# A transformer block on one core: the first modulation by strips of TensorE, one weight ring, and an output projection that ends token tile by token tile

## The chip, the core and the metric

The kernel runs on one core of a Trainium2 chip. Its engines work side by side and wait for one another through semaphores: TensorE (PE, with its weight loads PEld), VectorE (DVE), ScalarE (ACT), GpSimd (POOL) and SyncE (SP), whose queue issues most of the DMAs. The metric is the device time of one execution in microseconds (us); less is better.

## The reference

One layer over 512 latent tokens `x` and 256 context tokens `ctx`, width 1024, all in float32. Cut to what the change touches:

```python
m_lat = (silu(c) @ mod_w + mod_b)[:, None, :]        # conditioning of the latent tokens
m_ctx = silu(c_ctx) @ mod_w + mod_b                  # and of the context tokens
sh1, sc1, g1, sh2, sc2, g2 = split(m_lat, 6)         # six sections of 1024 columns
csh1, csc1, cg1, csh2, csc2, cg2 = split(m_ctx, 6)
h_lat = rms_norm(x, norm_mix_g) * (1 + sc1) + sh1
h_ctx = rms_norm(ctx, norm_mix_g) * (1 + csc1) + csh1
z_lat, z_ctx = h_lat @ w_in, h_ctx @ w_in            # then two mixers (gated DeltaNet "A", HGRN2 "B"), four heads each, both directions: ya, yb; the gates m_a, m_b
y = (sigmoid(m_a) * (ya @ w_up_a) + sigmoid(m_b) * (yb @ w_up_b)) @ w_out
x = x + g1 * y
h = rms_norm(x, norm_ffn_g) * (1 + sc2) + sh2
gate, up = split(h @ ffn_w_in, 2)                    # 2816 columns each
x = x + g2 * ((silu(gate) * up) @ ffn_w_out)
return rms_norm(x, final_norm_g)
```

## The kernel before

Everything on TensorE has 128 partitions. The 512 latent tokens are four token tiles of 128, the width is KT = 8 tiles `d`. Activations lie transposed (features on partitions, tokens in columns). To keep float32 accuracy, both operands of a large product are split into a high and a low half (`hi`, `lo`; `hhi`, `hlo` for the latent tokens, `chi`, `clo` for the context) and multiplied in three matmuls by `mm3` (L105). `split` fetches a weight by SP's queue into `raw`, ScalarE casts it to `hi` (L95), VectorE subtracts to get `lo` (L97); each ring of such tiles has two buffers.

The order on each engine is set by a scheduler that follows the order of the code and priorities written in it (`tc.cur_priority`), and by the rings of buffers that tiles share.

**Start.** SP's queue fetches the tiles of `mod_w` (`mw`, one for each d, with shift and scale columns, 512 bytes a run), x, and the first six column tiles of `w_in` (`wr`). `norm_rows` takes the norm of the tokens. `modulation(d, s)` computes the shift and the scale of feature tile d for s = 0 (latent) or s = 1 (context): VectorE multiplies the 8 rows of tiles by the conditioning and adds them into two `macc` (L264, L266), TensorE sums over partitions by four matmuls with a vector of ones into `pmod` (L270). `mod_columns` (L272) makes `mcol`. `prepare(d)` transposes x on TensorE (`px`, L283), ScalarE applies `mcol` (L285 for `hhi`, L287 for `hf`), VectorE makes `hlo` (L288) and `wl` (L300). Then 18 matmuls `pg` for each d (L316). The six `pg` banks are gates 16 to 21; gates 22 and 23 follow (`pgate`, 24 matmuls each), and beside them `modulation(d, 1)` for the context. After them come the context's tokens (`chi`, `clo`), the small projection `pab` (L369), and from `h_z` on the mixers' heads.

**Mixers.** A written plan orders the heads. `head_norm` (L419) squares a head's output on ScalarE, scales the sum `h_ss` on VectorE (L423), raises it to the power -0.5 on POOL (L426), applies it on ScalarE (L428) and transposes on TensorE (`h__pt`, L431). In this part the other sections of the modulation are computed in `mod_quarter`: POOL's queue fetches `mwb`, VectorE adds into `acc` (L829). They and the last gates have a later priority.

**After the mixers.** `branch` and `up` make the up-projections (`pup`), whose merge gives `mh`, `ml`. The output projection `pwo` has two halves of 512 columns, each with four banks (one for each token tile g). The contraction is four weight pieces kk: two are multiplied for all token tiles, the last two token tile by token tile. Then the residual (`xt`, L1015, `x1`, L1016), its square (L1017), the norm's scale `st` (L1022 to L1024), `xn` (L1026), transposes `px` (L1030) and `hhi`, `hlo` again (L1034 to L1038). SwiGLU follows: 22 tiles f of 128 columns of gate and up (`pf`), 48 matmuls each; f = 0 runs on two halves of 256 tokens, so that it can begin on token tiles 0 and 1. The last product is `pfo`.

Of the kernel before, what the change touches and what calls it, by code (L numbers as in the profile page):

```python
# [7 lines left out]
F32 = mybir.dt.float32  # L8
# [7 lines left out]
KT = 8  # L16
# [32 lines left out]
def body(tc, T, out, tap=None):  # L49
# [8 lines left out]
    with ExitStack() as root:  # L58
# [25 lines left out]
        def split(srcs, kt, n, pool=None):  # L84
# [5 lines left out]
            for s in srcs:  # L90
                w = s.shape[1]
                nc.sync.dma_start(raw[:, :, c0:c0 + w], s.rearrange("(k p) f -> p k f", p=P))
                c0 += w
            hi = pool.tile([P, kt, n], F32R, name=f"hi{WN[0]}", tag="hi")
# [59 lines left out]
        with ExitStack() as st:  # L154
# [32 lines left out]
            def load_mod(d):  # L187
                mw = s1.tile([P, KT, 256], F32, name=f"mw{d}")
                for j in range(2):
                    nc.sync.dma_start(mw[:, :, P * j:P * j + P],  # L190
                                      T["mod_w"][0, :, D * j + P * d:D * j + P * d + P].rearrange("(k p) f -> p k f", p=P))
                mws.append(mw)

            load_mod(0)
            for g in (2, 3, 4, 5):
                load_x(g)
            for d in range(KT):
                if d > 0:
                    load_mod(d)
                wr = s1.tile([P, NG0 * P], F32, name=f"wr{d}", tag="wr", bufs=3)  # L200
                nc.sync.dma_start(wr[:, :], W_IN[P * d:P * d + P, C_MB:C_MB + NG0 * P])
                wraws.append(wr)
# [39 lines left out]

            ss = s1.tile([P, 6], F32, name="ss")
# [14 lines left out]
            def modulation(d, s):  # L258

                accs = [sp.tile([P, 256], F32, name=f"macc{d}_{s}{i}", tag=f"macc{i}", bufs=4) for i in range(2)]  # L260
                for k in range(KT):
                    acc, col = accs[k % 2], sc[:, 8 * s + k:8 * s + k + 1]
                    if k < 2:
                        nc.vector.tensor_scalar_mul(acc[:, :], mws[d][:, k, :], col)  # L264
                    else:
                        nc.vector.scalar_tensor_tensor(acc[:, :], mws[d][:, k, :], col, acc[:, :], op0=ALU.mult, op1=ALU.add)  # L266
                for j in range(2):
                    c = 16 * s + 2 * d + j
                    for i, acc in enumerate(accs):
                        nc.tensor.matmul(pmod0[:, c:c + 1], acc[:, P * j:P * j + P], ones[:, 0:1], start=(i == 0), stop=(i == 1))  # L270

            def mod_columns(s, d0, d1):  # L272

                ps = pmod0[:, 16 * s + 2 * d0:16 * s + 2 * d1].rearrange("p (d j) -> p d j", j=2)
                nc.vector.tensor_tensor(mcol[:, s, d0:d1, 0], ps[:, :, 0], mb_sh[:, d0:d1], op=ALU.add)
                nc.vector.tensor_tensor(mcol[:, s, d0:d1, 1], ps[:, :, 1], mb1[:, d0:d1], op=ALU.add)
                nc.vector.tensor_tensor(mcol[:, s, d0:d1, 1], mcol[:, s, d0:d1, 1], g_mix[:, d0:d1], op=ALU.mult)
# [13 lines left out]
            pmod0 = bank("ha", "pmod0")  # L291
# [28 lines left out]
            norm_rows((0, 1))  # L320
            cd = list(range(KT))
# [803 lines left out]
```

## Time and profile before

| what | value |
|---|---|
| median of 3 runs (lowest to highest) | 1096.97 us (1096.02 to 1098.99) |
| profiled execution | 1099.97 us |
| its span | 1098.3 us |
| mean granted TensorE clock | 0.983 |
| TensorE busy | 1034.3 us |
| VectorE / ScalarE / GpSimd busy | 699.2 / 554.6 / 75.7 us |

The span runs from the first to the last recorded instruction. Between the start of x's first projection and the end, the program passes these edges (us from the start of the span): 67.9 the gates, 100.2 the mixers, about 610 the up-projections, 659.3 the output projection, 704.7 the transposes for SwiGLU, 737.0 its third tile. Times in the prediction are those of the profiled execution; it lies 3.0 us above the median.

### The profile page before, as it was taken

The numbers are of one execution on the slowest core, as the hardware profiler recorded it, in microseconds if no ns is written. First come the engines' busy times: TensorE is split into PE (matmuls) and PEld (weight loads), VectorE is DVE, ScalarE is ACT, GpSimd is POOL, SyncE is SP. The second block draws the span as 40 slices with busy tenths as digits, with TensorE's granted clock in tenths as the row PEclk, the third lists the DMA queues.
The fourth block names the chain that finished last, engine by engine and source line by source line (L and its number), as shares of the span: only waits on it lengthen the run. The fifth ranks groups of instructions, "written<-read, shape, count | busy, mean of one in ns | idle before, by whom it ended". The sixth has DMA issues, their size and how long they took to land.

```text
span 1098.3 us, 16604 instructions
## 1 busy us (share of the span) xinstructions
PE 1034.3 (94%) x6439; PEld 856.0 (78%) x6439; DVE 699.2 (64%) x1373; ACT 554.6 (50%) x1042; POOL 75.7 (7%) x132
## 2 busy tenths in 40 slices
PE   4999999979899999999989999999999999999996
PEld 3787788858797877789777787788888878888785
DVE  5896876789867967976796575686433333322524
ACT  3454578757877765887764743442222222221212
POOL 0010000220002022001111000110000000000000
PEclk9998999999999999999999999999999999999998
DMA  9943412122004213200728843454333323322222
GB/s 304 283 145 126 135 44 72 51 76 67 3 10 143 61 48 87 58 3 28 221 90 269 275 152 127 129 170 152 96 96 97 96 77 96 96 96 95 84 92 94
DMA packets 142721, 122.06 MB, mean 111 GB/s; under 512 B 5533, under 2 KB 118451, under 8 KB 142643
## 3 DMA queue, kind: packets, MB, share of 16 engines
q1 hardware_dynamic: 135907, 100.20, 30.0%
q0 software_dynamic: 4640, 17.30, 4.7%
q10 hardware_dynamic: 2096, 3.50, 0.9%
q8 instruction: 50, 0.82, 0.3%
q14 instruction: 28, 0.23, 0.1%
HBM read 110.51 MB, written 10.49 MB: 110 GB/s over the span
## 4 chain that ended last, share of the span: by engine, by line
PE 70%; DVE 12%; ACT 6%; issue 5%; DMA 4%; POOL 3%; SPq 0%; POOLq 0%; ACTq 0%; DVEq 0%
PE pf L105 22%; PE pfo L105 10%; PE pgate L105 5%; PE pup L105 4%; PE pg L316 3%; PE h_z L105 3%; PE pwo L105 3%; DVE lo L97 2%; PE h_zv L105 2%; PE p_s_pk L795 1%; PE pmod L270 1%; PE h_pA L482 1%; PE g_k_zl L105 1%; PE p_s_pk L786 1%; DMA mwb<-in_mod_w_dram 1%
## 5 line engine op out<-in xcount | busy, mean ns | idle before, releaser
L95 ACT CAST hi<-raw 128x1024 fp32r<-128x1024 f32 (+1 forms) x137 | 135.8, 992 | 310.1 <-PE pf L105 169.9
L97 DVE TENSOR_TENSOR lo<-raw,hi 128x1024 fp32r<-128x1024 f32 (+1 forms) x137 | 157.8, 1152 | 183.3 <-ACT hi L95 183.0
L105 PE MATMUL pf<-hhi,lo 128*128 128x512 f32 (+1 forms) x368 | 142.8, 389 | 0.4 <-DVE lo L97 0.4
L105 PE MATMUL pf<-hlo,hi 128*128 128x512 f32 (+1 forms) x368 | 142.8, 389 | 0.3 <-DVE hlo L1038 0.3
L105 PE MATMUL pf<-hhi,hi 128*128 128x512 f32 (+1 forms) x368 | 142.4, 389 | 0.0
L105 PEld LDWEIGHTS pf<-hhi,lo 128*128 128x128 f32 x368 | 70.2, 191 | 16.0 <-DVE lo L97 1.2
L105 PEld LDWEIGHTS pf<-hlo,hi 128*128 128x128 f32 x368 | 70.1, 191 | 15.3 <-DVE hlo L1038 0.5
L105 PEld LDWEIGHTS pf<-hhi,hi 128*128 128x128 f32 x368 | 69.9, 191 | 14.7
L105 PE MATMUL pfo<-lo,uh 128*128 128x512 f32 x176 | 69.8, 396 | 0.1
L105 PE MATMUL pfo<-hi,ul 128*128 128x512 f32 x176 | 69.5, 395 | 0.0
L105 PE MATMUL pfo<-hi,uh 128*128 128x512 f32 x176 | 68.7, 395 | 0.0
L105 PE MATMUL pgate<-hhi,lo 128*128 128x512 f32 x144 | 61.0, 424 | 6.2 <-DVE lo L97 6.2
L105 PE MATMUL pgate<-hhi,hi 128*128 128x512 f32 x144 | 60.5, 420 | 1.9 <-ACT hi L95 1.9
L105 PE MATMUL pgate<-hlo,hi 128*128 128x512 f32 x144 | 59.4, 413 | 0.0
L1061 DVE TENSOR_TENSOR sg<-sg,pf 128x512 f32<-128x512 f32 x22 | 15.1, 687 | 51.6 <-PE pf L105 51.5
L829 DVE SCALAR_TENSOR_TENSOR acc<-mwb,sc,acc 128x256 f32<-128x256 f32 x72 | 34.4, 482 | 10.1 <-DMA mwb<-in_mod_w_dram 8.9
L266 DVE SCALAR_TENSOR_TENSOR macc<-mw,sc,macc 128x256 f32<-128x256 f32 x96 | 39.9, 476 | 0.0
L105 PEld LDWEIGHTS pfo<-lo,uh 128*128 128x128 f32 x176 | 33.2, 188 | 8.6 <-DVE lo L97 1.0
L105 PEld LDWEIGHTS pgate<-hhi,lo 128*128 128x128 f32 x144 | 28.8, 200 | 13.8 <-DVE lo L97 8.6
L105 PEld LDWEIGHTS pfo<-hi,uh 128*128 128x128 f32 x176 | 32.9, 188 | 8.0 <-ACT hi L95 0.6
L105 PEld LDWEIGHTS pfo<-hi,ul 128*128 128x128 f32 x176 | 33.2, 188 | 7.6
L105 PE MATMUL h_z<-hhi,hi 128*128 128x512 f32 x96 | 38.1, 397 | 0.4 <-ACT abT L370 0.3
(426 smaller groups left out, 2523.0 us busy)
## 6 DMA issues: line engine op xcount, KB each, us to landing
raw<-in_ffn_w_in_dram SPq DMA_DIRECT2D x44, 512.0 KB, 3.8
raw<-in_w_in_dram SPq DMA_DIRECT2D x37, 512.0 KB, 3.9
raw<-in_ffn_w_out_dram SPq DMA_DIRECT2D x22, 512.0 KB, 3.5
mwb<-in_mod_w_dram POOLq DMA_DIRECT2D x18, 512.0 KB, 4.6
mw<-in_mod_w_dram SPq DMA_DIRECT2D x16, 512.0 KB, 6.2
mwe<-in_mod_w_dram POOLq DMA_DIRECT2D x7, 1024.0 KB, 6.2
gdram<-gt SPq DMA_DIRECT2D x24, 256.0 KB, 2.1
raw<-in_w_in_dram SPq DMA_DIRECT2D x18, 256.0 KB, 3.2
```

The costliest lines, as they stand in the source:

```text
L95: nc.scalar.copy(hi[:, :, :], raw[:, :, :])
L97: nc.vector.tensor_tensor(lo[:, :, :], raw[:, :, :], hi.bitcast(F32), op=ALU.subtract)
L105: nc.tensor.matmul(ps, a[u](k), b[v](k), start=(start and n == 0), stop=(stop and n == tot - 1))
L266: nc.vector.scalar_tensor_tensor(acc[:, :], mws[d][:, k, :], col, acc[:, :], op0=ALU.mult, op1=ALU.add)
L270: nc.tensor.matmul(pmod0[:, c:c + 1], acc[:, P * j:P * j + P], ones[:, 0:1], start=(i == 0), stop=(i == 1))
L316: nc.tensor.matmul(pg0[i][:, :], u[:, P * i:P * i + P], v[:, d, :], start=(d == 0 and n == 0), stop=(d == KT - 1 and n == 2))
L482: nc.tensor.matmul(pA[:, P * c:P * c + P], kq[:, 0, P * c:P * c + P], kq[:, 1, P * c:P * c + P], start=True, stop=True)
L786: nc.tensor.matmul(pk[:, P:2 * P], N[:, d, e, g, :], rt[:, :], start=True, stop=True)
L795: nc.tensor.matmul(pk[:, 2 * P:3 * P], kend[:, :], u[:, :], start=True, stop=True)
L829: nc.vector.scalar_tensor_tensor(acc[:, :], mw[:, k - k0, :], sc[:, k:k + 1], acc[:, :], op0=ALU.mult, op1=ALU.add)
L1061: nc.vector.tensor_tensor(sg[:, :], sg[:, :], pgu[1][:, :], op=ALU.mult)
```

## The change

It has four parts.

1. *Modulation by strips.* `mw` becomes eight chunks [128, 4, 512] (one quarter of the shift and scale columns, half of the rows; 1 KB a run; ring of six), and x goes out ahead of them. `modulation(q)` works on two tiles d for latent and context tokens at once: four fp32 matmuls for each half, whose stationary operand `sch` has 32 columns (two of them not zero) and whose outputs lie in four strips of 32 partitions of one bank (`tile_position=(0, 32 * k)`, L279 of the new kernel). VectorE copies the bank to `mr`; four matmuls with `comb` (L284) add the strips and bring features onto partitions; three VectorE operations make `mcol`. `macc` and its sums, and the context's separate modulation, are gone. `norm_rows((0, 1))`, the context's norm, is called at d = 6.
2. *One weight ring.* The pool "wp" lives from start to end and takes the place of "wf"; the late gates get a temporary ring "wx" on the right side of the memory. `yp` and `mg` lie where the early pools were; `yh`, `yl` have a tag for each branch.
3. *Output projection.* Half 0 is computed plainly, all four kk, then its residuals. For half 1, the four weight pieces are split into the memory of `yh0`, `yl0`, `yh1`, `yl1`, and the token tiles are finished one after another; `norm(tp)` follows each pair.
4. *SwiGLU.* f = 0 and f = 1 both run on halves of 256 tokens: first half of both, second half of both. f = 1's weights have tiles of their own (`w1ij`), whose memory `g2b` and `fgb` use later; `fgb` is fetched after them.

The diff, cut to its core:

```diff
@@ pools
-        ring = {"w": early.enter_context(pool("wp", 2))}
+        ring = {"w": root.enter_context(pool("wp", 2))}
...
-        wf = root.enter_context(pool("wf", 2, side="right"))
...
+        gx = ExitStack()
+        wx = gx.enter_context(pool("wx", 2, side="right"))
...
-                gate(gates.pop(0), ring["mod"], wf, "ga")
+                gate(gates.pop(0), ring["mod"], wx, "ga")
...
+        gx.close()
...
-        ring["w"] = wf
-        with pool("mg", 1) as mg:
+        with pool("yp", 1) as yp, pool("mg", 1) as mg:
@@ start
+                mw = s1.tile([P, 4, 512], F32, name=f"mw{c}", tag="mw", bufs=6)
                 for j in range(2):
+                    c0 = D * j + 256 * (c // 2)
+                    nc.sync.dma_start(mw[:, :, 256 * j:256 * j + 256],
+                                      T["mod_w"][0, 512 * (c % 2):512 * (c % 2) + 512, c0:c0 + 256].rearrange("(k p) f -> p k f", p=P))
...
-            load_mod(0)
             for g in (2, 3, 4, 5):
                 load_x(g)
             for d in range(KT):
+                load_mod(d)
+                if d % 2 == 0:
+                    continue
+                for e in (d - 1, d):
+                    wr = s1.tile([P, NG0 * P], F32, name=f"wr{e}", tag="wr", bufs=5)
...
+            sch = s1.tile([P, KT, 32], F32, name="sch")
+            nc.gpsimd.memset(sch[:, :, :], 0.0)
+            nc.vector.tensor_copy(sch[:, :, 0:2], sc.rearrange("p (s k) -> p k s", s=2))
...
+            def modulation(q):
+                ps = bank("ha", f"pmod{q}")
+                for half in range(2):
+                    for k in range(4):
+                        nc.tensor.matmul(ps[32 * k:32 * k + 32, :], sch[:, 4 * half + k, :], mws[2 * q + half][:, k, :],
+                                         start=(half == 0), stop=(half == 1), tile_position=(0, 32 * k))
+                mr = s1.tile([P, 512], F32, name=f"mr{q}", tag="mr", bufs=2)
+                nc.vector.tensor_copy(mr[:, :], ps[:, :])
+                for i in range(4):
+                    nc.tensor.matmul(ps[:, 2 * i:2 * i + 2], mr[:, P * i:P * i + P], comb[:, :], start=True, stop=True)
...
-            modulation(0, 0)
-            mod_columns(0, 0, 1)
+            modulation(0)
             prepare(0)
-            modulation(1, 0)
             for d in range(KT):
-                if d + 2 < KT:
-                    modulation(d + 2, 0)
+                if d % 2 == 0 and d + 2 < KT:
+                    modulation(d // 2 + 1)
                 if d + 1 < KT:
-                    mod_columns(0, d + 1, d + 2)
                     prepare(d + 1)
+                if d == 6:
+                    norm_rows((0, 1))
...
-            norm_rows((0, 1))
-            cd = list(range(KT))
             for i in rest[0:2]:
                 gate(i, sp)
-                for _ in range(8):
-                    if cd:
-                        modulation(cd.pop(0), 1)
-            for d in cd:
-                modulation(d, 1)
-            mod_columns(1, 0, KT)
@@ output projection
-                    for kk in range(2):
-                        w = split([T["w_out"][0, 256 * kk:256 * kk + 256, cs]], 2, 512)
-                        for g in range(4):
-                            part(w, kk, g)
-                    ws = [split([T["w_out"][0, 256 * kk:256 * kk + 256, cs]], 2, 512) for kk in (2, 3)]
-                    for g in range(4):
-                        for w, kk in zip(ws, (2, 3)):
-                            part(w, kk, g)
...
+                for kk in range(4):
+                    w = weights(0, kk)
+                    for g in range(4):
+                        part(0, w, kk, g)
+                for g in range(4):
+                    residual(0, g)
+                ws = []
+                for kk, tag in enumerate(("yh0", "yl0", "yh1", "yl1")):
+                    wt = yp.tile([P, 2, 2, 512], F32R, name=f"wo{kk}", tag=tag)
+                    ws.append(weights(1, kk, dst=(wt[:, 0, :, :], wt[:, 1, :, :])))
+                for tp in range(2):
+                    for g in (2 * tp, 2 * tp + 1):
+                        for kk in range(4):
+                            part(1, ws[kk], kk, g)
+                        residual(1, g)
+                    norm(tp)
@@ SwiGLU
+            w01 = ffn_weights(0), ffn_weights(1, [[t[:, :, :] for t in p] for p in w1])
+            for t0 in (0, 256):
+                for f in range(2):
+                    ffn_in(f, w01[f], t0, 256)
```

How this moves instructions is seen at three places. First TensorE at the start, around the end of the first d. Before, the column sums `pmod` of single feature tiles stand between the `pg`:

```order
L316 MATMUL pg_2_206<-hlo,wh_227 128x512
L270 MATMUL pmod_203<-ones,macc_00_240 128x1
L316 MATMUL pg_3_207<-hlo,wh_227 128x512
L316 MATMUL pg_4_208<-hlo,wh_227 128x512
L270 MATMUL pmod_203<-ones,macc_01_241 128x1
L270 MATMUL pmod_203<-ones,macc_00_240 128x1
L270 MATMUL pmod_203<-ones,macc_01_241 128x1
L316 MATMUL pg_5_209<-hlo,wh_227 128x512
L270 MATMUL pmod_203<-ones,macc_00_254 128x1
L270 MATMUL pmod_203<-ones,macc_01_255 128x1
L270 MATMUL pmod_203<-ones,macc_00_254 128x1
L270 MATMUL pmod_203<-ones,macc_01_255 128x1
```

After, TensorE has the strips of a half (`32x512 x4`), transposes for the next d, and, further down, the four combining matmuls:

```order
L299 MATMUL px_299<-sq,xt_108 128x128
L279 MATMUL pmod_247<-mw_131,sch 32x512 x4
L299 MATMUL px_299<-sq,xt_110 128x128
L299 MATMUL px_299<-sq,xt_112 128x128
L330 MATMUL pg_3_213<-hhi,wh_265 128x512
L330 MATMUL pg_4_214<-hhi,wh_265 128x512
L330 MATMUL pg_5_215<-hhi,wh_265 128x512
L284 MATMUL pmod_247<-comb,mr_256 128x2 x4
L330 MATMUL pg_0_210<-hhi,wl_266 128x512
L330 MATMUL pg_1_211<-hhi,wl_266 128x512
L330 MATMUL pg_2_212<-hhi,wl_266 128x512
L330 MATMUL pg_3_213<-hhi,wl_266 128x512
```

The column sums of a feature tile came singly, four in a call for each d and each s; now one quarter (two d, both s) comes as two groups of four strips and one group of four combining matmuls, and three of the four quarters stand behind the first `pg`.

Second, VectorE at the end of the last mixer head. `h2_ss` is the sum that this head's norm waits for; `mwb420` and `mwb424` are the two tiles of one quarter of the modulation. Before:

```order
L829 SCALAR_TENSOR_TENSOR acc42_5744<-mwb420_5746,sc_173,acc42_5744 128x256
L97 TENSOR_TENSOR lo49_5810<-raw49_5806,hi49_5808 128x1024
L829 SCALAR_TENSOR_TENSOR acc42_5744<-mwb420_5746,sc_173,acc42_5744 128x256 x3
L829 SCALAR_TENSOR_TENSOR acc42_5744<-mwb424_5752,sc_173,acc42_5744 128x256
L423 TENSOR_SCALAR h2_ss_6290<-h2_ss_6290 128x4
L829 SCALAR_TENSOR_TENSOR acc42_5744<-mwb424_5752,sc_173,acc42_5744 128x256 x3
L829 SCALAR_TENSOR_TENSOR acc43_5758<-mwb430_5760,sc_173,acc43_5758 128x256
```

After:

```order
L835 SCALAR_TENSOR_TENSOR acc41_5523<-mwb414_5531,sc_173,acc41_5523 128x256
L835 SCALAR_TENSOR_TENSOR acc42_5571<-mwb420_5573,sc_173,acc42_5571 128x256
L102 TENSOR_TENSOR lo57_6260<-raw57_6256,hi57_6258 128x1024
L835 SCALAR_TENSOR_TENSOR acc42_5571<-mwb420_5573,sc_173,acc42_5571 128x256
L429 TENSOR_SCALAR h2_ss_6117<-h2_ss_6117 128x4
L835 SCALAR_TENSOR_TENSOR acc42_5571<-mwb420_5573,sc_173,acc42_5571 128x256 x2
L835 SCALAR_TENSOR_TENSOR acc42_5571<-mwb424_5579,sc_173,acc42_5571 128x256 x4
```

`h2_ss` moved ahead of every sum on `mwb424`; what stands ahead of it now is the second sum on `mwb420` and the low half `lo57`, which stood elsewhere.

Third, TensorE at the end of the output projection (`wo0` to `wo3` are the four weight pieces of half 1, `pwo12` the bank of token tile 2, `xn0`, `xn1` the normed token tiles 0 and 1). Before, all transposes stand behind the last `pwo`:

```order
L105 MATMUL pwo13_6960<-hi73_7029,mh_6316 128x512
L105 MATMUL pwo13_6960<-lo73_7031,mh_6316 128x512
L105 MATMUL pwo13_6960<-hi73_7029,ml_6317 128x512
L1030 MATMUL px200_7115<-sq_91,xn0_7108 128x128
L1030 MATMUL px200_7115<-sq_91,xn1_7113 128x128
L1030 MATMUL px201_7122<-sq_91,xn0_7108 128x128
L1030 MATMUL px201_7122<-sq_91,xn1_7113 128x128
L1030 MATMUL px202_7129<-sq_91,xn0_7108 128x128
```

After, those of token tiles 0 and 1 stand among the matmuls of token tile 2:

```order
L110 MATMUL pwo12_6633<-wo0_6779,ml_6147 128x512
L110 MATMUL pwo12_6633<-wo1_6784,mh_6146 128x512 x2
L110 MATMUL pwo12_6633<-wo1_6784,ml_6147 128x512
L110 MATMUL pwo12_6633<-wo1_6784,mh_6146 128x512 x2
L110 MATMUL pwo12_6633<-wo1_6784,ml_6147 128x512
L110 MATMUL pwo12_6633<-wo2_6789,mh_6146 128x512 x2
L110 MATMUL pwo12_6633<-wo2_6789,ml_6147 128x512
L1034 MATMUL px200_6869<-sq_91,xn1_6867 128x128
L1034 MATMUL px201_6876<-sq_91,xn1_6867 128x128
L1034 MATMUL px202_6883<-sq_91,xn1_6867 128x128
L110 MATMUL pwo12_6633<-wo2_6789,mh_6146 128x512 x2
L110 MATMUL pwo12_6633<-wo2_6789,ml_6147 128x512
```

The transposes of `xn1` have the 16 `pwo` of token tile 2 that stand ahead of them as the only matmuls since token tile 1's last; those of `xn3` stand, in the same way, among the first half-width `pf`.

More of the change, by code (lines that the diff above doesn't have):

```diff
@@ L82, in body, with split @@
         WN = [0]
-        def split(srcs, kt, n, pool=None):
+        def split(srcs, kt, n, pool=None, dst=None):
             WN[0] += 1
@@ L93, in split @@
                 c0 += w
+            if dst is not None:
+                hi, lo = dst
+                nc.scalar.copy(hi, raw[:, :, :])
+                nc.vector.tensor_tensor(lo, raw[:, :, :], hi.bitcast(F32), op=ALU.subtract)
+                return hi, lo
             hi = pool.tile([P, kt, n], F32R, name=f"hi{WN[0]}", tag="hi")
@@ L241, in body @@
             nc.vector.tensor_scalar_add(mb1[:, :], mb_sc, 1.0)
+            sch = s1.tile([P, KT, 32], F32, name="sch")
+            nc.gpsimd.memset(sch[:, :, :], 0.0)
+            nc.vector.tensor_copy(sch[:, :, 0:2], sc.rearrange("p (s k) -> p k s", s=2))
+            comb = s1.tile([P, 2], F32, name="comb")
+            nc.vector.tensor_tensor(comb[:, :], ident[:, 0:2], ident[:, 32:34], op=ALU.add)
+            for j in (64, 96):
+                nc.vector.tensor_tensor(comb[:, :], comb[:, :], ident[:, j:j + 2], op=ALU.add)
             ss = s1.tile([P, 6], F32, name="ss")
@@ L256, in body @@
             mcol = s1.tile([P, 2, 8, 2], F32, name="mcol")
[L258 to L270, printed above, removed]
@@ L993, in body @@
+            merge_a = up(0, T["w_up_a"][0], branch(0))
+            next(merge_a)
+            yb = branch(1)
+            for _ in merge_a:
+                pass
+            mod_sums()
+            md.close()
+            row_bcast(g1b, mbc[:, 16:24], "ga")
+            nc.vector.scalar_tensor_tensor(A2[:, :], mbc[:, 32:40], 1.0, g_ffn, op0=ALU.add, op1=ALU.mult)
+            for _ in up(1, T["w_up_b"][0], yb):
+                pass
             with pool("xp", 2) as xp:
@@ L995, in body @@
                 for half in range(2):
-                    cs = slice(512 * half, 512 * half + 512)
                     for g in range(4):
                         pss[half, g] = bank(QUAD[half][g], f"pwo{half}{g}")
-                    def part(w, kk, g):
-                        mm3(pss[half, g][:, :], [lambda k, t=t: t[:, 2 * kk + k, P * g:P * g + P] for t in (mh, ml)],
-                            [lambda k, t=t: t[:, k, :] for t in w], 2, start=(kk == 0), stop=(kk == 3))
-                    for kk in range(2):
-                        w = split([T["w_out"][0, 256 * kk:256 * kk + 256, cs]], 2, 512)
-                        for g in range(4):
-                            part(w, kk, g)
@@ L1018, in body, with part, weights, residual @@
-                xn = {}
-                for tp in range(2):
+                def part(half, w, kk, g):
+                    mm3(pss[half, g][:, :], [lambda k, t=t: t[:, 2 * kk + k, P * g:P * g + P] for t in (mh, ml)],
+                        [lambda k, t=t: t[:, k, :] for t in w], 2, start=(kk == 0), stop=(kk == 3))
+                def weights(half, kk, **kw):
+                    return split([T["w_out"][0, 256 * kk:256 * kk + 256, 512 * half:512 * half + 512]], 2, 512, **kw)
+                def residual(half, g):
+                    cs = slice(512 * half, 512 * half + 512)
+                    xr = xp.tile([P, 512], F32, name=f"xr{half}{g}", tag="xr")
+                    nc.scalar.dma_start(xr[:, :], T["x"][0, P * g:P * g + P, cs])
+                    t = xp.tile([P, 512], F32, name=f"xt_{half}{g}", tag="xt_")
+                    nc.vector.tensor_tensor(t[:, :], pss[half, g][:, :], g1b[:, cs], op=ALU.mult)
+                    nc.vector.tensor_tensor(x1[:, g, cs], t[:, :], xr[:, :], op=ALU.add)
+                    nc.scalar.activation(t[:, :], x1[:, g, cs], AF.Square, accum_out=st2[:, 2 * g + half:2 * g + half + 1])
@@ L1020, in body, with norm @@
+                def norm(tp):
+                    xn = {}
                     for g in (2 * tp, 2 * tp + 1):
```

133 lines of the change are left out of this document (58 added, 75 removed).

## The prediction

> **What bounds the kernel now.** I read the page first, then the table of stretches, then the timeline at the edges of the stretches that the change touches.
>
> ```profile
> span 1098.3 us, 16604 instructions
> PE 1034.3 (94%) x6439; PEld 856.0 (78%) x6439; DVE 699.2 (64%) x1373; ACT 554.6 (50%) x1042; POOL 75.7 (7%) x132
> GB/s 304 283 145 126 135 44 72 51 76 67 3 10 143 61 48 87 58 3 28 221 90 269 275 152 127 129 170 152 96 96 97 96 77 96 96 96 95 84 92 94
> PE 70%; DVE 12%; ACT 6%; issue 5%; DMA 4%; POOL 3%; SPq 0%; POOLq 0%; ACTq 0%; DVEq 0%
> ```
>
> TensorE is busy 94% of the span and holds 70% of the chain that ends last. (The GB/s row is what the DMA moved in 40 equal slices.) So only two things shorten this kernel: TensorE work taken away, and the few stretches in which TensorE waits. The stretches the change touches (busy time and count for PE, PEld, DVE, ACT, POOL, then the granted clock, DMA share, GB/s):
>
> ```profile
> 19.60:68.10 48.50, 46.58 (x229) 38.76 (x230) 41.82 (x114) 22.85 (x33) 1.38 (x2) 0.96 0.81 224
> 68.10:90.80 22.70, 21.13 (x120) 18.43 (x118) 19.98 (x57) 6.46 (x9) 1.94 (x2) 0.86 0.70 232
> 90.80:100.10 9.30, 8.41 (x42) 5.49 (x42) 5.18 (x15) 8.24 (x19) 0.32 (x6) 0.78 0.40 113
> 583.00:610.00 27.00, 24.72 (x103) 19.58 (x102) 15.75 (x25) 17.44 (x27) 2.05 (x2) 0.94 0.85 279
> 659.30:704.70 45.40, 45.34 (x193) 35.56 (x192) 21.58 (x31) 13.16 (x22) 1.14 (x2) 1.00 0.39 128
> 704.70:737.00 32.30, 28.94 (x177) 25.51 (x176) 28.08 (x58) 18.61 (x35) 4.92 (x7) 0.95 0.49 146
> ```
>
> In the first three, TensorE looks full, but it is full of many small passes, and VectorE (41.82 of 48.5) paces it. From h_z (100.16, below) to the end of the mixers TensorE's order is unchanged; I carry no change there.
>
> **The first modulation.** Removed: VectorE's sums (L264, L266) and TensorE's column sums (L270).
>
> ```profile
> L266 DVE SCALAR_TENSOR_TENSOR macc<-mw,sc,macc 128x256 f32<-128x256 f32 x96 | 39.9, 476 | 0.0
> L270 PE MATMUL pmod<-ones,macc 128*128 128x1 f32 x128 | 17.2, 252 | 6.0 <-DVE macc L266 6.0
> L482 PE MATMUL h_pA<-h_kq 128*128 128x128 f32 x224 | 32.3, 280 | 0.7 <-DVE h_kq L507 0.4 <-ACT h_kq L506 0.2
> L111 PE MATMUL g_k_pn<-ones,g_k_acc 128*32 128x1 f32 x192 | 2.3, 172 | 0.6 <-ACT g_k_acc L625 0.6
> ```
>
> The code has 64 matmuls on L270, the row 128: an fp32 matmul is two passes. The timeline from the first pg to h_z (start, duration, instruction, idle before it and who ended it):
>
> ```profile
> 18.85 0.78 ACT L285 ACTIVATE hhi<-px,mcol 128x512 fp32r<-128x512 f32 x1 [3.65 <-PE px L283]
> 19.68 0.80 PE L316 MATMUL pg<-hhi,wh 128*128 128x512 f32 x1 [0.87 <-ACT hhi L285]
> 30.11 1.22 PE L316 MATMUL pg<-hhi,wh 128*128 128x512 f32 x2 [1.54 <-ACT hhi L285]
> 61.13 1.53 PE L316 MATMUL pg<-hhi,wl 128*128 128x512 f32 x6
> 62.50 1.52 PE L316 MATMUL pg<-hlo,wh 128*128 128x512 f32 x6
> 67.94 0.39 PE L105 MATMUL pgate<-hhi,hi 128*128 128x512 f32 x1
> 73.39 3.63 PE L270 MATMUL pmod<-ones,macc 128*128 128x1 f32 x32
> 76.88 0.48 PE L105 MATMUL pgate<-hhi,hi 128*128 128x512 f32 x1
> 90.82 0.56 ACT L285 ACTIVATE chi<-px,mcol 128x256 fp32r<-128x256 f32 x1 [3.91 <-DVE mcol L277]
> 100.16 0.50 PE L105 MATMUL h_z<-hhi,hi 128*128 128x512 f32 x1 [0.31 <-ACT abT L370]
> 140.22 0.40 PE L105 MATMUL pgate<-hlo,hi 128*128 128x512 f32 x1
> 140.54 0.58 PE L111 MATMUL g_k_pn<-ones,g_k_acc 128*32 128x1 f32 x48
> ```
>
> Six pg take 62.50−61.13 = 1.37, so 0.228 each. A column-sum pass takes (76.88−73.39)/32 = 0.109.
>
> Price of a strip. No fp32 matmul of 512 columns stands in the trace. L482 (128 columns, 280 ns) against L111 (one column, 172 ns) gives 108/127 = 0.85 ns a column: 0.44 us a pass, 0.88 us a matmul. Four strips one after another are 3.5 us; side by side, 0.9 to 1.0. The nearest row is L111, whose outputs are 32 columns wide too: 48 passes in (0.58−0.17)/48 = 0.0085 each, thirteen times quicker than L270's 0.109. A quarter of the weight columns would explain four times; the other factor of three is strips at work together. I take 0.95 for a group of four and keep 3.5 as the other end. The Trainium skill, "TensorE: Matmul & The Clock Gate", Part 3, measured three column strips with 512 columns at 2.38 times one after another, not 3 times. My estimate from that ratio is 3.5/3.2 = 1.1 for four, which would add 0.9 us over six groups; L111's row, with one column, can't tell the two apart.
>
> Start: x now goes out first and two mw chunks (1 MB) precede a matmul. Before, hhi at 18.85 waited for x's transposes, not for mcol, so x paced the start. x now leaves without 0.5 MB ahead of it: 1.6 us sooner at the first slice's 304 GB/s; the second chunk lands as much later than x did before, and its strips, copy, combining and three small operations then stand on the path. First pg at 19.6, ±1.
>
> From there: 144 pg × 0.228 = 32.8; 28 transposes × 0.109 = 3.1; six groups of strips × 0.95 = 5.7; 12 combining matmuls of two passes × 0.109 = 2.6. Entering the strips' shape cost 140.54−140.22−0.228 = 0.09; with as much for leaving, 12 changes are 1.1, and I take 1.5. Before, the wait at 30.11 was followed by a clock below 1 (0.96 in the stretch, 4% of 48.5 = 1.9); I keep 1.7. The sum is 47.4: the gates start at 67.0 (before: 67.94). VectorE loses L266's 39.9 us and the multiplies of L264, and gains four copies of 512 columns and small operations, so it no longer paces.
>
> Next, 48 gate matmuls × 0.228 = 10.9 bring 77.9. The context's modulation is done by then; its norm stands at d = 6, where VectorE now has room. I allow 1.0 for a weight cast that ScalarE has ahead; then the chain from the first chi to h_z keeps 100.16−90.82 = 9.3. So h_z at 88.5 to 89.5 against 100.16: **−11**. Bounds: −13 (no cast ahead, no switching), +5 (strips one after another: six groups cost 15 us more). The Trainium skill, "TensorEngine Tiling (Array Packing)", Key Properties, says that a change of tiling mode drains TensorE, which speaks against this change. By L111's 0.09 such a drain is inside my 1.5; twelve drains of a whole 0.17 tail would be 2.0, half a microsecond more.
>
> **The weight ring and the mixers' end.** VectorE's order changes where the last head's norm waits:
>
> ```profile
> 583.41 0.48 DVE L829 SCALAR_TENSOR_TENSOR acc<-mwb,sc,acc 128x256 f32<-128x256 f32 x1 [2.29 <-DMA mwb<-in_mod_w_dram]
> 583.81 0.16 DVE L423 TENSOR_SCALAR h_ss<-h_ss 128x4 f32<-128x4 f32 x1
> 584.05 1.25 POOL L426 TENSOR_TENSOR h_ss<-h_ss,mhalf 128x4 f32<-128x4 f32 x1 [1.90 <-DVE h_ss L423]
> 585.76 0.33 PE L431 MATMUL h__pt<-sq,h_on 128*128 128x128 f32 x1 [2.28 <-ACT h_on L428]
> ```
>
> h_ss stood behind an acc that waited 2.29 for its mwb; TensorE then idled 2.28, and its clock fell (0.94 over 27 us: 1.6 lost). After, h_ss stands behind the acc of an earlier mwb and one lo of 1024 columns. All back: −3.9. Same wait for another mwb: 0; a second one: +2. The lo (about twice L1015's 0.69 for 512 columns, below: 1.3) eats part: I take **−2**. The later accs wait instead, and only the end of the modulation needs them.
>
> Weights of the up-projection load earlier into the shared ring. Before, TensorE waited once for them:
>
> ```profile
> 616.05 0.40 PE L105 MATMUL pup<-yl,hi 128*128 128x512 f32 x1
> 616.98 0.50 PE L105 MATMUL pup<-yh,lo 128*128 128x512 f32 x1 [0.53 <-DVE lo L97]
> ```
>
> 0.93−0.23 = **−0.7**, 0 if SP's queue holds the raws as late as before.
>
> **Output projection to the third SwiGLU tile.** The same matmuls, in another order:
>
> ```profile
> 699.30 0.69 DVE L1015 TENSOR_TENSOR xt<-pwo,g1b 128x512 f32<-128x512 f32 x1 [0.45 <-PE pwo L105]
> 700.03 0.69 DVE L1016 TENSOR_TENSOR x<-xt,xr 128x512 f32<-128x512 f32 x1
> 700.81 0.63 ACT L1017 ACTIVATE xt<-x 128x512 f32<-128x512 f32 x1 [1.20 <-DVE st L1023]
> 702.58 0.56 POOL L1024 TENSOR_TENSOR st<-st,mhalf 128x1 f32<-128x1 f32 x1 [1.12 <-DVE st L1023]
> 703.17 0.75 DVE L1026 TENSOR_SCALAR xn<-x,st 128x1024 f32<-128x1024 f32 x1 [0.67 <-POOL st L1024]
> 707.97 0.44 PE L1030 MATMUL px<-sq,xn 128*128 128x128 f32 x2 [2.45 <-ACT hhi L1037]
> 708.82 0.28 PE L105 MATMUL pf<-hhi,lo 128*128 128x256 f32 x1
> 708.94 0.28 PE L105 MATMUL pf<-hhi,hi 128*128 128x256 f32 x1
> ```
>
> The third SwiGLU tile begins at 737.0, where the last stretch in the table ends: 77.7 us from the first pwo at 659.3. The work: 192 pwo and 48 pf × 0.23 = 55.2, 96 half-width pf × 0.12 = 11.5, 32 transposes × 0.109 = 3.5; together 70.2. So 7.5 were lost: the 2.45, smaller waits, and the clock (0.95 of 32.3). After, f=1 is halved too; work as before. The chain from a token tile's last pwo to its transpose is 0.69+0.69+0.63+0.56+0.75 and some 1.2 of small steps and hand-overs: 4.5 us. For the second tile of each pair only 16 pwo (3.7) and 26 half-width pf (3.1) stand between in TensorE's order; for the first ones, 24 and more (5.5). I count 1.0 for each of the second tiles plus VectorE's queue (0.8 and 0.5 for a weight's lo), and 2.2 for transposes that wait for their bank while ScalarE turns out its pieces of 256 columns (0.56 each, as chi's): 5.5. **−2**; bounds −5.5 (nearly all hidden), +2 (four waits of 2.45). No wait is then long enough for a clock drop.
>
> Sum: −11 −2 −0.7 −2 = −15.7 on the profiled execution's 1099.97: 1084.3. It lies 3.0 above the median of 1096.97, so against that: 1081.3.
>
> **Rivals.** (1) Strips overlap in part, 2 us a group: +6.5, 1088; for it, that L111's row shows strips with a single column only. (2) The output projection's transposes stall TensorE: 1081.3 plus 4 to 7.5 (its upper bound and a clock drop), 1085 to 1089; against it, the 16 and 26 matmuls of cover. (3) Strips do not overlap: 3.5 a group, +15.3: 1097, no change. (4) Slower: strips one after another while TensorE is granted half clock, because groups break up its dense stretch: 7 a group, 36 more than forecast: 1117. It decides from 3.4 us a group upward. The stretch 90.80:100.10 at 0.78 shows that sparse work does lose the clock; dense pg around the groups speak against it.
>
> **Chances.** Forecast 0.64 (its own range 1075 to 1086: the start ±1, and the ends of the later terms, −5.5 and +4); (1) 0.13; (2) 0.09; (3) 0.08; (4) 0.06. The range 1075 to 1091 holds the forecast's case and (1) and (2), less their tails. What measures no change from a difference is 0.3%, 3.3 us: faster (below 1093.7) 0.85, same 0.09 with (3), slower 0.06 with (4).
>
> **What would show it.** Strips right: L279's groups 0.9 to 1.1 us from start to start of the next matmul; wrong from 2 us. The start right: first pg near 19.6, the gates from 67, h_z near 89 and no wait of ScalarE for mcol before chi. The mixers' end right: h__pt waits under 1 us and the clock stays at 1. The output projection right: no gap over 1.5 us ahead of L1034, third tile 75 to 76 us after the first pwo. I would be wrong most of all by the strips, which no row of this profile shows at 512 columns.

## The result and the profile after

| | median of runs | ratio to before (95% interval) |
|---|---|---|
| before | 1097.98 us (1096.02 to 1099.42) | |
| after | 1082.01 us (1078.14 to 1082.95) | 0.9843 (0.9825 to 0.9862) |

The forecast was 1081 (1075 to 1091). The sum holds, but two of its terms promised some 4 us each that did not come, and a term of some 10 us was missing. The page of the changed kernel begins with these two lines; those of the page before stand in the prediction:

```profile
span 1079.6 us, 16501 instructions
PE 1014.1 (94%) x6455; PEld 839.9 (78%) x6455; DVE 656.5 (61%) x1238; ACT 554.5 (51%) x1042; POOL 76.6 (7%) x133
```

TensorE is as full as before (94%) and its busy time fell by 20.2 us, a little more than the span (18.7), though it runs 16 more passes. VectorE lost 42.7 us. The timeline of TensorE up to the second strips, then the edges of the stages:

```profile
13.25 1.93 PE L279 MATMUL pmod<-mw,sch 128*32 128x512 f32 x8 [7.43 <-DVE xt L270]
16.22 1.20 PE L279 MATMUL pmod<-mw,sch 128*32 128x512 f32 x8 [0.21 <-DMA mw<-in_mod_w_dram]
21.42 2.93 PE L330 MATMUL pg<-hhi,wh 128*128 128x512 f32 x6 [2.13 <-ACT hhi L301]
24.14 2.76 PE L330 MATMUL pg<-hhi,wl 128*128 128x512 f32 x6
38.00 1.06 PE L279 MATMUL pmod<-mw,sch 128*32 128x512 f32 x8
38.99 0.66 PE L299 MATMUL px<-sq,xt 128*128 128x128 f32 x4
70.39 0.39 PE L110 MATMUL pgate<-hhi,hi 128*128 128x512 f32 x1
81.28 0.81 PE L299 MATMUL px<-sq,xt 128*128 128x128 f32 x6
93.45 0.50 PE L110 MATMUL h_z<-hhi,hi 128*128 128x512 f32 x1 [0.32 <-ACT abT L376]
577.09 0.33 PE L437 MATMUL h__pt<-sq,h_on 128*128 128x128 f32 x1 [1.11 <-ACT h_on L434]
```

A group of four strips (eight passes) takes 38.99−38.00 = 0.99 us. The first two groups are slower (1.9 and 1.1). The first begins at 13.25; the second waits for its chunk of mw until 16.22, and the first pg is 5.2 us behind that. The first 12 matmuls of pg run at 0.45 each, 2.7 us for six from 21.42 to 24.14; the granted clock was 0.50 there.

The same stages in both profiled executions (first instruction of the stage on TensorE, in us), against the forecast's terms:

| stage | before | after | change | forecast |
|---|---|---|---|---|
| start to first pg | 19.7 | 21.4 | +1.7 | −0.1 |
| pg | 48.3 | 49.0 | +0.7 | −0.9 |
| gates 22, 23, context, to h_z | 32.2 | 23.1 | −9.1 | −10 |
| mixers, to the last h__pt | 485.6 | 483.6 | −2.0 | −2 with the next line |
| to the first pup | 24.4 | 23.0 | −1.4 | |
| up-projections | 49.1 | 52.2 | +3.0 | −0.7 |
| pwo to the third SwiGLU tile | 77.7 | 74.9 | −2.8 | −2 |
| third tile to the end | 361.3 | 352.5 | **−8.8** | 0 |

The last line is the surprise: the matmuls of that stretch are the same in both kernels, and what differs for them is the place of tiles. (The granted clock also fell to 0.50 from 897.0 to 900.4 in the trace of before, and not in that stretch of after; that is up to 1.7 of the 8.8.) Two stretches of 100 us in it, one of pf and one of pfo, as a table of windows (busy time and number of PE's instructions, granted clock, DMA share, GB/s), before and then after:

```profile
770.00:870.00 100.00, 100.00 (x432) 1.00 0.32 94
960.00:1060.00 100.00, 99.94 (x430) 1.00 0.27 91
```

```profile
770.00:870.00 100.00, 100.00 (x443) 1.00 0.34 100
960.00:1060.00 100.00, 99.92 (x439) 1.00 0.27 92
```

Both are full, both at clock 1.00, and yet 443 matmuls fit where 432 did: 100/432 = 231 ns each against 100/443 = 226 ns. The medians from start to start are 232 and 227. So each 512-column matmul became about 5.5 ns quicker; from the first pup to the end there are some 1900 of them, 10 us.

### The profile page after: what moved, and what is told of

It is laid out like the page before. It is cut to its first block, busy times and chain, and to the rows that moved or that the text cites. A ratio compares the mean times of both kernels' runs of the same rounds, so it can differ in the third digit from the quotient of the medians.

```text
span 1079.6 us, 16501 instructions
## 1 busy us (share of the span) xinstructions
PE 1014.1 (94%) x6455; PEld 839.9 (78%) x6455; DVE 656.5 (61%) x1238; ACT 554.5 (51%) x1042; POOL 76.6 (7%) x133
## 4 chain that ended last, share of the span: by engine, by line
PE 60%; DVE 13%; DMA 9%; ACT 7%; issue 7%; POOL 3%; SPq 0%; POOLq 0%; ACTq 0%; DVEq 0%
PE pf L110 20%; PE pfo L110 10%; PE pg L330 3%; PE pup L110 3%; PE h_z L110 3%; PE pgate L110 2%; DMA mwb<-in_mod_w_dram 2%; DVE lo L102 2%; DMA mwe<-in_mod_w_dram 2%; PE h_zv L110 2%; DMA ug<-gdram 1%; ACT hi L100 1%; DMA gdram<-gt 1%; PE p_s_pk L801 1%; PE g_k_zl L110 1%
## 5 line engine op out<-in xcount | busy, mean ns | idle before, releaser
L100 ACT CAST hi<-raw 128x1024 fp32r<-128x1024 f32 (+1 forms) x131 | 129.7, 991 | 279.9 <-PE pf L110 97.3
L102 DVE TENSOR_TENSOR lo<-raw,hi 128x1024 fp32r<-128x1024 f32 (+1 forms) x131 | 150.5, 1150 | 172.6 <-ACT hi L100 172.2
L110 PE MATMUL pf<-hhi,lo 128*128 128x512 f32 (+1 forms) x352 | 133.8, 380 | 0.8 <-DVE lo L102 0.8
L110 PE MATMUL pf<-hhi,hi 128*128 128x512 f32 (+1 forms) x352 | 133.8, 381 | 0.0
L110 PE MATMUL pf<-hlo,hi 128*128 128x512 f32 (+1 forms) x352 | 133.7, 380 | 0.0
L110 PEld LDWEIGHTS pf<-hhi,lo 128*128 128x128 f32 x352 | 66.2, 188 | 13.7 <-DVE lo L102 1.2
L110 PEld LDWEIGHTS pf<-hlo,hi 128*128 128x128 f32 x352 | 66.2, 188 | 12.5 <-DVE hlo L1042 0.2
L110 PEld LDWEIGHTS pf<-hhi,hi 128*128 128x128 f32 x352 | 66.1, 188 | 12.5
L110 PE MATMUL h_z<-hhi,lo 128*128 128x512 f32 x96 | 38.0, 396 | 0.0
```

Source lines behind the costliest of these rows:

```text
L100: nc.scalar.copy(hi[:, :, :], raw[:, :, :])
L102: nc.vector.tensor_tensor(lo[:, :, :], raw[:, :, :], hi.bitcast(F32), op=ALU.subtract)
L110: nc.tensor.matmul(ps, a[u](k), b[v](k), start=(start and n == 0), stop=(stop and n == tot - 1))
```

## The experiments

Runs e1 to e4 share a chip, e5 to e8 another, e9 to e11 a third; each chip has its own runs of before (medians 1099.84, 1101.65, 1101.16), so ratios are compared and not times.

**e1 and e2: where the weight tiles begin.** In the built programs, hhi begins 96 bytes past a multiple of 256. The late ring of before ("wf") begins 224 past one, the ring after 96. The edit of e1, on the kernel before:

```diff
+        padp = root.enter_context(pool("padp", side="right"))
+        pad = padp.tile([P, 32], F32, name="pad")
+        nc.gpsimd.memset(pad[:, :], 0.0)
         wf = root.enter_context(pool("wf", 2, side="right"))
```

> The kernel before with one edit: 128 bytes are set aside ahead of the late weight ring, so that its tiles begin 96 bytes past a multiple of 256 (as hhi and the early ring do) rather than 224. In the traces, 512-column fp32r matmuls follow each other at 232 ns before and at 227 ns after, from the late gates to the end. Theory A (where tiles begin decides): the cadence becomes 227 from the late gates on; about 2000 matmuls at 5.5 ns give -11 us, some 1086. Theory B (the ring's region, its side, or that it is shared with the start decides): cadence stays 232 and the time stays at 1097. Theory C (the two profiled executions merely ran at different clocks): no change, 1097.

Measured: 1090.08, ratio 0.9906 (0.9871 to 0.9941). The same stretches of e1:

```profile
770.00:870.00 100.00, 100.00 (x443) 1.00 0.33 95
960.00:1060.00 100.00, 99.94 (x440) 1.00 0.28 95
```

443 and 440, against 443 and 439 in the changed kernel: with 128 unused bytes the kernel before gets the last line of the table (352.7 us from the third tile to the end). Theory A is right, and the ring's region (e1's ring lies where wf lay), its side or its sharing is not the cause. e2 does the reverse to the changed kernel (the same three lines with `pool("padp")` ahead of the ring "wp", which moves everything above it too).

> The changed kernel with the opposite edit: 128 bytes between hpool and the weight ring, so that the ring, the up-projection's tiles, mh, ml, uh and ul all begin 224 past a multiple of 256, while hhi and hlo stay at 96. Theory A, absolute form (a tile at 224 is slow): every 512-column fp32r matmul with such a tile runs at 232, some 2736 of them, +15 us, 1097. Theory A, relative form (stationary and moving operand 128 bytes apart are slow): pg, the heads' projections and pf slow down (1824 matmuls, +10 us, 1092), pup, pwo and pfo, both of whose operands lie at 224, stay at 227. Theories B and C: 1082.

Measured: 1085.81, ratio 0.9861 (0.9828 to 0.9894).

```profile
770.00:870.00 100.00, 100.00 (x432) 1.00 0.33 95
960.00:1060.00 100.00, 99.94 (x440) 1.00 0.29 99
```

pf, with stationary weights at 224 and moving hhi at 96, is back at 432. pfo, whose weights and whose uh, ul now all lie at 224, stays at 440. So it is the difference between the two operands that costs, not the place of one: the relative form. pup and pwo, both operands at 224, also stayed at 227 ns, and pg and h_z slowed to 232. The span grew by 6.4 rather than the 10 expected: the stretch from the third tile on took 5.0 more, the mixers 2.8, and the up-projections 1.6 less. The times alone would not tell e2 from the changed kernel (0.9843; the intervals overlap); the spacing of the matmuls does.

**e7: the smallest step.** 32 bytes instead of 128.

```diff
+        padp = root.enter_context(pool("padp"))
+        pad = padp.tile([P, 8], F32, name="pad")
+        nc.gpsimd.memset(pad[:, :], 0.0)
         ring = {"w": root.enter_context(pool("wp", 2))}
```

> The changed kernel with 32 bytes between hpool and the weight ring, so that hhi and the ring's tiles differ by 32 modulo 256 (128 gave 232.4 ns, 64 and 192 of the gates' small ring 230 to 233, 0 gave 227). If any difference costs: pf's cadence is 229 to 233 and its 1056 matmuls take 3 to 6 us more. If only a part of the address counts (from 64 bytes up): 227, no change. pfo, both operands moved alike, stays at 227 either way.

One run: 1087.62.

```profile
770.00:870.00 100.00, 100.00 (x431) 1.00 0.33 95
960.00:1060.00 100.00, 99.93 (x440) 1.00 0.29 99
```

pf is back at 431, pfo stays at 440: a difference of 32 bytes costs as much as one of 128.

**e3: strips one after another.**

```diff
-                        nc.tensor.matmul(ps[32 * k:32 * k + 32, :], sch[:, 4 * half + k, :], mws[2 * q + half][:, k, :],
-                                         start=(half == 0), stop=(half == 1), tile_position=(0, 32 * k))
+                        nc.tensor.matmul(ps[0:32, :], sch[:, 4 * half + k, :], mws[2 * q + half][:, k, :],
+                                         start=(half + k == 0), stop=(half + k == 4), tile_position=(0, 0))
...
-                    nc.tensor.matmul(ps[:, 2 * i:2 * i + 2], mr[:, P * i:P * i + P], comb[:, :], start=True, stop=True)
+                    nc.tensor.matmul(ps[:, 2 * i:2 * i + 2], mr[0:32, P * i:P * i + P], ident[0:32, 0:2], start=True, stop=True)
```

> The changed kernel with the eight strip matmuls of a quarter all put into the first strip of 32 partitions, one accumulation, with the combining matmuls on 32 partitions; the result is the same. Theory (the four strips work side by side, the group of four took 1.0 us): a group of four now takes 3.5 us; eight groups, 20 us more on TensorE, of which the first two lie partly behind the wait for mw: +15 to +18, about 1099. Rival (a matmul with 32 weight columns is cheap whatever its place, and side by side explains little): groups stay near 1 us, 1082.

Measured: 1095.37, ratio 0.9956 (0.9939 to 0.9973). One quarter, sixteen passes, on its timeline:

```profile
24.73 7.03 PE L279 MATMUL pmod<-mw,sch 128*32 128x512 f32 x16 [0.37 <-PE pmod L284]
31.69 0.55 PE L299 MATMUL px<-sq,xt 128*128 128x128 f32 x3
```

6.96 us for two groups of four, 0.43 a pass, where the changed kernel takes 0.99 for a group. Four strips at four places thus work side by side, 3.5 times as fast as at one place. The span is 14.0 longer and h_z 14.6 later, a little less than the 15 to 18 expected (the first two quarters, which in e3 stand ahead of the first pg, lie partly beside x's norms).

**e5: strips alone.** The kernel before with the changed code from the fetch of mw to the context's tokens, nothing else.

```diff
+                mw = s1.tile([P, 4, 512], F32, name=f"mw{c}", tag="mw", bufs=6)
...
-            modulation(0, 0)
-            mod_columns(0, 0, 1)
+            modulation(0)
```

> The kernel before with the first modulation of the changed kernel alone (strips, mw in chunks behind x, the context's norm at d = 6); weight rings, output projection and SwiGLU as before, so the late ring stays 128 bytes off against hhi. From the traces: h_z came at 93.45 in the changed kernel and at 100.16 before. Theory (the start's gain is its own, and passes through the mixers unchanged): -6.7 us, some 1091 where before gives 1098; the late cadence stays at 232. Rival (the start's gain is partly the weight ring's doing, since the ring is shared): less than 4 us.

Measured: 1093.93, ratio 0.9935 (0.9914 to 0.9957), 0.65% or 7.1 us. In its trace h_z came at 92.96, 7.2 earlier than before, and the end of TensorE's work 6.0 earlier; pup, pwo, pf and pfo stay at 232 ns. The theory holds: the start has its gain without the ring, and most of it reaches the end.

**e4: the dropped tile.** Beside its four parts, the change dropped a tile of the up-projections, `us`: the gated product is written over `uy`. e4 puts it back into a tile of its own.

```diff
+                    sg = yp.tile([P, SEQ], F32, name=f"us{br}{h}", tag="us", bufs=2)
...
-                    nc.vector.tensor_tensor(yt[:, :], gt[:, :], yt[:, :], op=ALU.mult)
-                    nc.scalar.copy(yh[:, h, :], yt[:, :])
+                    nc.vector.tensor_tensor(sg[:, :], gt[:, :], yt[:, :], op=ALU.mult)
+                    nc.scalar.copy(yh[:, h, :], sg[:, :])
```

> The changed kernel with the dropped tile us back: the gated product goes into a tile of its own (2 buffers) and not over uy. In the changed kernel the up-projection waits 2.65 and 1.74 us for its PSUM banks, whose reader (the product with mg) waits for the gates' DMA. Theory (uy is held longer by the product in place, so later loads of ug, uy and mg move back in SP's queue): both waits go, -3.9 us, about 1078. Rival (the waits come from the order of SP's queue, in which the weights of the shared ring and the gates now stand, not from us): no change, 1082.

What TensorE waits for in the up-projections (us in total, times, longest; waits under 0.4 left out), in the kernel before, in the changed kernel and then in e4:

```profile
PE pup L105 <- DVE lo L97: 0.5, 1, 0.5
```

```profile
PE pup L110 <- DVE x L976: 3.6, 2, 2.3
PE pup L110 <- DVE lo L102: 0.4, 1, 0.4
```

```profile
PE pup L110 <- DVE x L977: 0.9, 2, 0.7
```

The waits for x (the product that reads the bank) shrink from 3.6 to 0.9, and the up-projections from 52.2 to 48.8 us. The other traces agree: with the changed kernel's up-projections and no us (e2, e3, e6, e7, e11) they took 50.5 to 51.7 us, with waits for x of 2.0 to 3.1; with us (e8, e10) they took 49.1 and 49.2, with 1.4 and 1.5. The time did not show it: 1082.01, ratio 0.9836 (0.9794 to 0.9878). In this one execution h_z came 2.1 later and the mixers took 2.3 us more than in the changed kernel's, with the same order of instructions; that is more than the gain. That the missing tile makes most of these waits is shown; what it is worth in the time is not shown by e4.

**e6: the old tail.** The changed kernel with the output projection and SwiGLU's first tile as before.

> The changed kernel with the output projection and the first SwiGLU tiles as before (parts c and d undone), ring and start as changed. From the first pwo to the third SwiGLU tile the aligned kernel before took 76.7 us and the changed one 74.9. Theory (the new order gains only what the late transposes cost before, less its own three waits of 1.99, 0.89 and 0.91): +1.8, some 1084. Rival (my forecast's term of 2, plus what the earlier fgb and g2b do to the DMA): +2 to +5. Third: nothing, 1082.

```diff
-                for tp in range(2):
-                    for g in (2 * tp, 2 * tp + 1):
-                        for kk in range(4):
-                            part(1, ws[kk], kk, g)
-                        residual(1, g)
-                    norm(tp)
+                    for g in range(4):
+                        for w, kk in zip(ws, (2, 3)):
+                            part(w, kk, g)
```

Measured: 1085.29, ratio 0.985 (0.9825 to 0.9874): not told apart from the changed kernel's 0.9843. In the trace, pwo to the third tile took 76.7 us, as in e1 (76.7) and against 74.9: the 1.8 that was expected. The chip's times neither confirm nor refute it. One more difference lies behind the third tile: from there to the end e6 took 356.1 us against 352.5. At 747.98 TensorE had waited 2.85 for a weight's lo, and the granted clock was then 0.50 for 3.4 us. e9 below, which also has the old tail, has the same wait (1.84) and the same fall of the clock; e1, with the old tail too, waits 1.1 and keeps its clock; the changed kernel's two traces wait 0.8 and 0.2. Whether the old tail makes this wait, no run shows.

**e8 and e10: a version with the waits mended.** Beside us and 64 bytes ahead of fl's tiles (which puts 216 gate matmuls at difference 0), the first token pair's norm is called behind token tile 2; e8 also fetches two chunks of mw ahead of x.

```diff
-                for tp in range(2):
-                    for g in (2 * tp, 2 * tp + 1):
-                        for kk in range(4):
-                            part(1, ws[kk], kk, g)
-                        residual(1, g)
-                    norm(tp)
+                for g in range(4):
+                    for kk in range(4):
+                        part(1, ws[kk], kk, g)
+                    if g == 2:
+                        norm(0)
+                    residual(1, g)
+                norm(1)
```

> The changed kernel with four edits: the first two mw chunks ahead of x; us back; 64 bytes in fl, so that its tiles too lie at 96 like hhi (216 matmuls); norm of the first token pair called behind token tile 2's matmuls rather than ahead of them. Expected from the traces: first pg 1.4 earlier (the chain from the second chunk's landing to pg, 5.2, is longer than that from x's last tile, 4.2); up to 3 from the up-projection's waits, of which e4 showed nothing in its time; 0.7 from fl; 2.5 from the waits of 1.99 and 0.89 in the output projection and their changes of shape. Sum -4 to -7: 1075 to 1078. Rival: the late transposes then stand close to SwiGLU's start and wait there for ScalarE: -2 at most, 1080.

e8: 1077.65, ratio 0.9789 (0.9767 to 0.9811). The sum is as expected, but not its first term: the first pg came at 23.2, not 20. x's four norms follow each other 1.5 us apart, so x's first tile and not its last sets the start, and h_z came at 96.6, later than in any execution with x first and the strips side by side (92.1 to 95.5). That edit was a mistake, and e10 undoes it. The 64 bytes ahead of fl brought nothing that the traces show: among the mixers, gate matmuls that stand in a row follow each other at 230 ns on average in e8 and e10, as in the changed kernel.

> e8 without its first edit: x leaves ahead of the mw chunks again, as in the changed kernel. In e8 the first pg came at 23.2 rather than 21.4, since x's four norms follow each other 1.5 us apart. Expected: first pg back at 21.4, h_z at 93.5 rather than 96.6, of which the mixers seemed to give back 2 to 3 us: 0 to -2 against e8, ratio to before 0.977 to 0.979. Rival (the later start is hidden anyway by the mixers): equal to e8.

e10: 1077.83, ratio 0.9798 (0.9775 to 0.9821); the first pg is at 21.3 and h_z at 93.9, but the time is e8's. By the traces the mixers return the difference: h_z is 2.8 apart and the last h__pt 0.7. That is what the rival said. In e10 the stretch from the first pwo to the third tile, in one row (busy time of PE, PEld, DVE, ACT, POOL), beside the changed kernel's:

```profile
649.00:722.50 73.50, 71.89 (x417) 62.21 (x417) 51.17 (x89) 33.54 (x58) 6.11 (x9) 1.00 0.45 138
```

```profile
652.20:727.00 74.80, 72.07 (x417) 61.80 (x416) 50.58 (x88) 33.66 (x58) 6.12 (x9) 1.00 0.44 137
```

**e9 and e11: what the change comes to.** e9 is the kernel before with e5's strips and e1's 128 bytes, nothing else; e11 is the changed kernel once more.

> The kernel before with two edits only: the first modulation by strips (as in e5) and 128 bytes ahead of the late weight ring (as in e1); no shared ring, no new output projection, no halved second SwiGLU tile. Theory (the change's whole gain is the strips and the place to which its layout happened to move the weight tiles; its other parts cancel): the ratios of e1 and e5 multiply, 0.9906 x 0.9935 = 0.984, as the changed kernel's 0.984: some 1081 where before gives 1098. Rival (the new tail and the ring bring 2 to 3 us of their own): 0.9865 or more, and clearly behind the changed kernel on the same chip.

> The changed kernel itself, unaltered, on the same chip as e9 and e10, so that they can be compared without a change of chip: ratio to before 0.984, first pg between 21 and 23, the stretch of the mixers within 2 us of the first profile.

e9: 1086.64, ratio 0.9873 (0.9842 to 0.9905). e11: 1082.57, ratio 0.9835 (0.9812 to 0.9857), with the first pg at 22.8 and the mixers 0.6 us from the first profile's, as expected. The two edits bring 1.27% of the changed kernel's 1.65%, over three quarters. The rest, about 4 us, is in favour of the rival, but the intervals overlap. In these traces e11 is 7.8 ahead at the end: 4.4 by the last h__pt (e9 has the old order on VectorE there), 2.7 between pwo and the third tile, and 3.3 in SwiGLU, where e9 waits 1.84 for a weight's lo and has the clock at 0.50 for 3.4 us; the up-projections and the gates ahead of them give 2.6 back. e10 is 0.4% ahead of e11 on the same chip (intervals meet at 0.9812 to 0.9821); it and e8 have the lowest ratios measured. Which of e10's edits makes its lead is not shown: its up-projections took 49.2 us against 51.7 in e11 and the stretch to the third tile 73.5 against 74.3, but the two profiled executions lie only 1.7 us apart where the medians lie 4.7.

## Why the prediction was right, and where only its sum was

**Strips: right.** I priced a pass at 0.44 and a group at 0.95; e3 shows 0.43 and the profile 0.99. Rivals 1, 3 and 4 fell with this (2, 3.5 and 7 us a group), and rival 2 with the tail below. The Trainium skill, "TensorE: Matmul & The Clock Gate", Part 3, gives 2.38 times for three column strips. My estimate of 3.2 times for four, worked out from it, was too low: this case's four strips run 3.5 times as fast as one after another (0.99 against 3.48 us).

**The start: mechanism right, size wrong (−6.7 for −11).** Three steps were too short. The first pg: I let x and the second chunk balance; the chunk landed at 16.2 and strips, copy, combining, mcol and hhi took 5.2 more (+1.8). In the eight other executions with this start, the first pg came between 21.2 and 23.1, against 19.7 in before and e1. In e11, the same kernel, it came at 22.8, because the second strips took 1.9 and the combining matmuls 1.87, where the first profile has 1.2 and 1.05. The clock: I kept 1.7 for a cold stretch (one at a low granted clock), but TensorE comes cold to the first pg (0.50 until 26.8), whose first twelve matmuls alone lose 12 x 0.22 = 2.6; with a wait of 0.40 for the second hhi, pg took 49.0 rather than my 47.4 (+1.6). And from the last gate matmul to h_z I took 10.3; it took 12.2 (+1.9), since a copy of a gate stands between ScalarE's first chi operation and its hf and itself waits:

```profile
82.65 0.57 ACT L301 ACTIVATE chi<-px,mcol 128x256 fp32r<-128x256 f32 x1
84.22 0.59 ACT L136 COPY gt<-pgate 128x512 f32<-128x512 f32 x1 [1.00 <-DMA gdram<-gt]
84.71 0.57 ACT L303 ACTIVATE hf<-px,mcol 128x256 f32<-128x256 f32 x1
```

The order showed that copy; I counted the weight cast ahead of chi and not the copy behind it. The three steps make 5.3, and not the 4.3 of the heading, because my terms add up to h_z at 88.2, below the 88.5 to 89.5 that I gave.

**The mixers' end: right, a little low.** −2 was forecast with all of −3.9 as the bound. The last h__pt now waits 1.11 instead of 2.28, just over the 1 us that I had set as the sign, and the clock holds (1.00 from there to the first pup, before 0.93):

```profile
575.13 0.17 DVE L429 TENSOR_SCALAR h_ss<-h_ss 128x4 f32<-128x4 f32 x1
575.38 1.25 POOL L432 TENSOR_TENSOR h_ss<-h_ss,mhalf 128x4 f32<-128x4 f32 x1 [1.05 <-DVE h_ss L429]
576.67 1.14 ACT L434 ACTIVATE h_on<-h_po,h_ss 128x128 f32<-128x128 f32 x4 [1.57 <-POOL h_ss L432]
579.22 1.01 DVE L835 SCALAR_TENSOR_TENSOR acc<-mwb,sc,acc 128x256 f32<-128x256 f32 x2 [2.96 <-DMA mwb<-in_mod_w_dram]
```

The wait for mwb that h_ss stood behind is now 2.96 long and stands behind it, where only the late sums need it. The table's two lines of the mixers give −3.4; some 2 us of the mixers also vary between executions of one order. From h_z to the first pup, the four executions with the old order (before, e1, e5, e9) took 509.6 to 512.6 us, and the seven with the new one and aligned weights (after, e3, e4, e6, e8, e10, e11) took 503.9 to 508.9. That the order of VectorE makes this difference is argued from the waits; no run changes this order alone.

**The up-projections: wrong sign (+3.0 for −0.7).** I looked at when the weights load and at nothing else in that stage, and even there a wait of 0.4 for a lo is left of the 0.5. The step that failed is that part of the working: us was dropped in the same stage, I did not cost it at all, and e4 shows the waits it makes (3.6 us with the change, 0.9 with us back).

**The tail: right.** −2 forecast, −2.8 measured, of which 1.0 is the shorter matmul; at equal offsets (e1 against after) 1.8. The shortfall of cover came at the second tiles as expected (0.50 and 0.63), but the longest wait, 1.60 for the xn of token tile 0, stood where I had counted enough cover, and it is just over my limit of 1.5.

```profile
687.30 0.44 PE L1034 MATMUL px<-sq,xn 128*128 128x128 f32 x2 [1.60 <-DVE xn L1030]
691.25 0.55 PE L1034 MATMUL px<-sq,xn 128*128 128x128 f32 x3 [0.50 <-DVE xn L1030]
704.94 0.55 PE L1034 MATMUL px<-sq,xn 128*128 128x128 f32 x3 [0.63 <-DVE xn L1030]
```

**Missing: the place of the tiles (−10).** The weight ring I costed by what its transfers do. What it did was to move the weights by 128 bytes against hhi, yh, mh and uh, which lie at 96 in both kernels. e1 shows what that is worth: 9.8 us between the medians (6 to 14 by the interval), with 128 bytes and nothing else. The trace before already held both times from start to start, and I used both without asking why: 0.228 for pg, 0.23 for pwo and pf.

That the total came out within 1 us is therefore luck: 7 to 8 us of forecast gains did not come, and 10 that I had not seen made up for them.

## What to carry to other kernels

Compare the start-to-start time of the same matmul in different stages of one trace: a per cent or two between full stretches at the same clock is a cause to find, and where tiles lie is one of them. Pad pools so that the stationary and the moving tiles of a long fp32r product begin at the same place modulo 256 bytes, and look at the addresses again after each change of a pool. When a change gives a total that fits, check it stage by stage all the same.

## What the runs showed of the hardware

A 512-column fp32r matmul with 128x128 weights takes 227 ns from start to start when its stationary and its moving operand begin at the same place modulo 256 bytes, and 232 to 233 on average when they differ by 32 (e7) or 128 (before, e2). A difference of 64 is not shown to cost: the gates' small ring gives 230 at 64 bytes off (after) and the same 230 at difference 0 (e8, e10), both in short rows of matmuls. The common place does not matter (96 in after, 224 for pfo in e2), nor the region (e1's ring at the upper end of the memory, differing from hhi by a multiple of 256 but not of 512, is as fast as the low ring). In the same traces transposes show no such difference (0.109 us with operands 0, 32, 64 or 96 bytes apart); for fp32 matmuls no run tests it. Which part of the memory or of TensorE causes it was not tried.

Four fp32 matmuls of 512 columns in four column strips take 0.99 us where the same four in one strip take 3.48 (half of e3's 6.96 for eight).
